# Strided attention on one Trainium2 core: longer read runs in the DMAs that load Q and store the output

## The chip, the cores and the metric

The kernel runs on one core of one Trainium2 chip. The metric is the device time of one execution in microseconds (us), as the median of several executions. The kernel before took 130.86 us (median of 3 runs, 130.84 to 131.28).

## The reference, cut to what matters

Every query attends to the 16 keys at positions 0, 64, 128, ... of its head. Q, K, V and the result are float32 of shape (8, 12, 1024, 64), so Q and the result are 25.17 MB each. Of K and V only one row in 64 is read.

```python
attend_positions = np.arange(0, seq, stride)          # stride = 64: 16 positions
k = K[:, :, attend_positions, :];  v = V[:, :, attend_positions, :]
scores = np.einsum('bhqd,bhkd->bhqk', q, k) / np.sqrt(dim)
weights = softmax(scores)                             # over the 16 keys
result[:, :, i, :] = np.einsum('bhqk,bhkd->bhqd', weights, v)
```

## The kernel before

The 96 heads are worked in 24 groups of four. A group's Q is 1 MiB: each of the 128 SBUF partitions gets 32 rows of 64 floats, 8 KiB in one piece. There are 11 buffers for Q and 9 for results. All 11 first loads are issued before any computing; from then on the program issues a store and a load in turn.

```python
QBUFS = 11
OBUFS = 9
# ... pools, constants, K and V: cut ...

def load(g):                       # 128 runs of 8 KiB, HBM and SBUF alike
    qn[g] = qn_pool.tile([P, 32 * D], FP32, name="qn", tag="qn")
    nc.sync.dma_start(qn[g], _ap_with(Q, [[32 * D, P], [1, 32 * D]], g * HG * SD))

for g in range(QBUFS):
    load(g)
# ... transposes (PE, evicted by ACT), scores (PE, exp by ACT), sums, outputs (PE, scaled by DVE): cut ...

def store(g):                      # 256 runs of 4 KiB, SBUF and HBM alike
    nc.sync.dma_start(
        _ap_with(out, [[16 * D, P], [2 * SD, 2], [1, 16 * D]], g * HG * SD),
        out_sb[g].rearrange("p b i x -> p b (i x)"),
    )

for g in range(NG):
    # ... sums(g), outputs(g, 0..3), scores(g + 1), transposes(g + 2): cut ...
    store(g)
    if g + QBUFS < NG:
        load(g + QBUFS)
```

A *run* here is one contiguous piece that one side of a DMA reads or writes. For a load the read side is HBM (the chip's main memory) and the write side is SBUF (the core's own memory, in 128 partitions); for a store it is the other way round. A *packet* is one record of the profiler for one piece of a DMA on one of the core's 16 DMA engines. PE, ACT and DVE are the engines that compute (matmul, activation, vector).

The softmax here doesn't subtract the row's maximum and nothing guards it: scores larger than these inputs give would overflow.

## Time and profile before

| what | before | where it is read |
|---|---|---|
| time, median | 130.86 us | timed runs |
| DMA data queue, share of 16 engines' span | 97.6% | part 3 of the page |
| ACT, DVE, PE busy | 67%, 65%, 55% | part 1 of the page |
| last byte moved | 127.8 us | DMA packet records |
| last DVE instruction ends | 114 us | timeline |

Lines of the page of the kernel before: the span; the busy share of the DMA engines in 40 slices, in tenths, and the GB/s of each slice; the packets by size; the data queue; the chain of waits by engine; two groups of instructions (busy us, mean ns); and the two kinds of DMA with the time from issue to landing.

```profile
span 129.1 us, 2215 instructions
...
DMA  2999999999999999999999999999999999999980
GB/s 64 273 426 416 419 431 419 421 411 421 415 423 433 405 428 426 414 425 420 419 428 420 416 435 419 419 431 415 420 434 404 420 417 417 419 420 421 420 360 34
DMA packets 13098, 51.26 MB, mean 397 GB/s; under 512 B 3872, under 2 KB 3872, under 8 KB 10016
...
q1 hardware_dynamic: 13088, 51.12, 97.6%
...
ACT 61%; PE 11%; DVE 5%; DMA 3%; issue 3%; POOL 3%; ACTq 1%; DVEq 0%; POOLq 0%
...
L223 DVE TENSOR_TENSOR out_sb<-o_ps,rec 128x512 f32<-128x512 f32 x96 | 63.2, 689 | 15.2 <-PE o_ps L218 12.8
L178 ACT COPY qt<-qt_ps 128x1024 bf16<-128x1024 bf16 x48 | 46.2, 1015 | 5.2 <-PE qt_ps L173 4.7
...
qn<-in_Q_dram SPq DMA_DIRECT2D x24, 1024.0 KB, 19.5
out_dram<-out_sb SPq DMA_DIRECT2D x24, 1024.0 KB, 19.2
```

The DMA row stands at 9 from slice 2 almost to the end: nothing else is full for so long. The chain of waits names ACT for 61%, but ACT and DVE are finished by 114 us while stores, issued 19 us ahead of their landing, are still draining.

Busy time by stage in the kernel before. Each line is one stretch: its limits and length, then busy us and instructions of each engine, granted TensorE clock, DMA share and GB/s.

```profile
core 0: us, PE busy (x) PEld busy (x) DVE busy (x) ACT busy (x) POOL busy (x), PEclk, DMA share, GB/s
12.00:24.00 12.00, 7.74 (x66) 5.50 (x65) 8.43 (x16) 6.63 (x8) 0.00 (x0) 0.88 1.02 424
60.00:95.00 35.00, 23.42 (x317) 17.48 (x315) 26.87 (x45) 30.19 (x37) 0.00 (x0) 1.00 1.02 423
112.00:122.00 10.00, 0.90 (x4) 0.22 (x2) 2.06 (x4) 0.00 (x0) 0.00 (x0) 0.50 1.02 420
```

The three stretches are the loads-only stage, the mixed stage and the stores-only stage. The DMA share is 1.02 in each. It can exceed 1 because the records of neighbouring packets overlap by about 4 ns: a 4 KiB packet's record lasts 159 ns, and the next packet of its engine starts after 155 ns (median).

These GB/s count a packet whole in the stretch in which it starts. That is coarse for long packets, so all rates from here on are worked out from the packet records of the data queue (q1), with each packet's bytes spread evenly over its recorded time. For the kernel before they are 421.8, 421.5 and 420.5 GB/s in these stretches. There was no idle engine to fill: from 12 to 122 us the records never show fewer than 16 packets under way. In that time a gain could come only from the pace, which was 155 ns from start to start for 4 KiB, and for 8 KiB 309 ns in the loads-only and 306 ns in the mixed stage (medians). How high the rate could go was not shown.

### The profile page before, as it was taken

To read this page: it belongs to the slowest core of one execution; us is meant where nothing else is said; L and a number is where in the kernel's file an instruction comes from. 1 tells how busy PE (TensorE), PEld (TensorE's weight loads), DVE (VectorE), ACT (ScalarE), POOL (GpSimd) and SP (SyncE) were. 2 spreads that over 40 slices of the span, in tenths; PEclk is the share of its full clock that TensorE was granted. 3 is DMA by queue.
4 is the path that set the end of the run, shared out by engine and by line. 5 is a ranking of instruction groups with operands and counts; after the bars stand their busy time and mean duration, and the time that the engine had idled before them with its cause. 6 is when DMAs were issued, how large, how long until landed. Compare 5 with 4: busy or idle time off the path is not lost.

```text
span 129.1 us, 2215 instructions
## 1 busy us (share of the span) xinstructions
PE 70.4 (55%) x880; PEld 51.8 (40%) x880; DVE 83.7 (65%) x144; ACT 86.2 (67%) x103; POOL 5.1 (4%) x23
## 2 busy tenths in 40 slices
PE   0071665986666776666866667856668765600000
PEld 0040542765444554445655445544456543300000
DVE  6229964787778777778777787777787777830000
ACT  2173294988889888889888899888898888200000
POOL 4460000000000000000000000000000000000000
PEclk9999997799999999999999999999999999555555
DMA  2999999999999999999999999999999999999980
GB/s 64 273 426 416 419 431 419 421 411 421 415 423 433 405 428 426 414 425 420 419 428 420 416 435 419 419 431 415 420 434 404 420 417 417 419 420 421 420 360 34
DMA packets 13098, 51.26 MB, mean 397 GB/s; under 512 B 3872, under 2 KB 3872, under 8 KB 10016
## 3 DMA queue, kind: packets, MB, share of 16 engines
q1 hardware_dynamic: 13088, 51.12, 97.6%
q8 instruction: 7, 0.11, 0.3%
q14 instruction: 3, 0.02, 0.0%
HBM read 25.95 MB, written 25.17 MB: 396 GB/s over the span
## 4 chain that ended last, share of the span: by engine, by line
ACT 61%; PE 11%; DVE 5%; DMA 3%; issue 3%; POOL 3%; ACTq 1%; DVEq 0%; POOLq 0%
ACT qt L178 34%; ACT w L198 27%; PE sc L186 8%; DVE v_bd L160 3%; DMA k_raw<-in_K_dram 3%; PE qt_ps L173 1%; DVE out_sb L223 1%; POOL k_dup L96 1%; PE o_ps L218 1%; POOL perm_v L100 1%; POOL v_bf L104 1%; ACTq L285 1%; PE sm L207 1%; DVEq L285 0%; PE vp L155 0%
## 5 line engine op out<-in xcount | busy, mean ns | idle before, releaser
L223 DVE TENSOR_TENSOR out_sb<-o_ps,rec 128x512 f32<-128x512 f32 x96 | 63.2, 689 | 15.2 <-PE o_ps L218 12.8
L178 ACT COPY qt<-qt_ps 128x1024 bf16<-128x1024 bf16 x48 | 46.2, 1015 | 5.2 <-PE qt_ps L173 4.7
L198 ACT ACTIVATE w<-sc 64x512 bf16<-64x512 f32 x48 | 35.3, 736 | 13.1 <-PE sc L186 12.8
L218 PE MATMUL o_ps<-v_bd,w 128*128 128x256 bf16 x192 | 34.2, 284 | 0.0
L173 PE MATMUL qt_ps<-identity,qn 128*128 128x128 bf16 x384 | 31.1, 228 | 0.2 <-ACT qt L178 0.2
L173 PEld LDWEIGHTS <-qn 128*128 128x128 bf16 x384 | 27.3, 103 | 3.9 <-issue 2.6
L186 PE MATMUL sc<-qt,k_t 128*32 128x512 bf16 x96 | 9.8, 396 | 24.3 <-ACT qt L178 24.3
L218 PEld LDWEIGHTS <-w 128*128 128x128 bf16 x192 | 14.6, 100 | 6.6 <-issue 5.6
L186 PEld LDWEIGHTS <-k_t 128*32 128x32 bf16 x96 | 4.4, 93 | 29.1 <-issue 29.0
L211 DVE RECIPROCAL rec<-sm 128x32 f32<-128x32 f32 x24 | 8.6, 358 | 9.0 <-PE sm L207 8.9
L207 PE MATMUL sm<-s_sel,w 128*128 128x4 bf16 x192 | 8.5, 166 | 6.7 <-ACT w L198 5.6
L207 PEld LDWEIGHTS <-w 128*128 128x128 bf16 x192 | 6.4, 96 | 10.8 <-ACT w L198 10.8
L160 DVE TENSOR_SCALAR v_bd<-vp,mask 128x384 bf16<-128x384 f32 x16 | 8.5, 608 | 0.1
L146 ACT CAST k_t<-kp 64x512 bf16<-64x512 f32 x6 | 3.5, 579 | 3.5 <-PE kp L140 3.4
L140 PE MATMUL kp<-perm_k,k_dup 128*128 128x128 bf16 x12 | 1.5, 312 | 6.6 <-POOL k_dup L96 6.6
L155 PE MATMUL vp<-v_bf,perm_v 128*128 128x384 bf16 x4 | 1.8, 491 | 4.6 <-DVE v_bd L160 4.1
L140 PEld LDWEIGHTS <-k_dup 128*128 128x128 bf16 x12 | 1.2, 145 | 6.6 <-POOL k_dup L96 6.6
L118 DVE TENSOR_SCALAR slot_i<-iota_p 128x1 int16<-128x1 int16 x1 | 0.2, 156 | 4.6 <-POOL iota_p L116 4.6
L146 ACT ACT_TABLE_LOAD x1 | 1.3, 1283 | 2.5 <-DVE k_t L107 2.5
L107 DVE MEMSET k_t<- 128x1536 uint32 x1 | 1.3, 1338 | 1.1 <-PEq L271 1.1
L155 PEld LDWEIGHTS <-perm_v 128*128 128x128 bf16 x4 | 0.5, 128 | 3.7 <-issue 3.7
L96 POOL CAST k_dup<-k_raw 128x768 bf16<-128x768 f32 x2 | 1.6, 827 | 3.0 <-DMA k_raw<-in_K_dram 3.0
(15 smaller groups left out, 6.0 us busy)
## 6 DMA issues: line engine op xcount, KB each, us to landing
qn<-in_Q_dram SPq DMA_DIRECT2D x24, 1024.0 KB, 19.5
out_dram<-out_sb SPq DMA_DIRECT2D x24, 1024.0 KB, 19.2
k_raw<-in_K_dram SPq DMA_DIRECT2D x1, 384.0 KB, 4.2
v_raw<-in_V_dram SPq DMA_DIRECT2D x1, 384.0 KB, 5.4
```

Source lines behind the costliest of these rows:

```text
L96: nc.gpsimd.tensor_copy(out=k_dup[:, :, e], in_=k_raw)
L140: nc.tensor.matmul(kp[:, i], lhsT=k_dup[:, 4 * n + i].rearrange("p e d -> p (e d)"), rhs=pk, start=True, stop=True,)
L146: nc.scalar.copy(k_t[h, 4 * n : 4 * n + 4, :, :, e].rearrange("p n c s k -> p (n c s) k"), kp[h].rearrange("p n c s k -> p (n c s) k"),)
L160: nc.vector.tensor_scalar(out=v_bd[:, 6 * n : 6 * n + 6, c, s], in0=vp, scalar1=mask[:, s : s + 1], scalar2=None, op0=ALU.mult,)
L173: nc.tensor.transpose(ps[:, i], _ap_with(qb, [qb.ap[0], [2, P]], extra_offset=(8 * x + i) * 2 * P + 1), identity,)
L178: nc.scalar.copy(qt[g][:, x], ps)
L186: nc.tensor.matmul(sc[32 * j : 32 * j + 32], lhsT=kt[:, 32 * j : 32 * j + 32], rhs=_ap_with(q, [q.ap[0], [P, 8], [8 * P, 2], [1, 32]], ext ...
L198: nc.scalar.activation(out=_ap_with(wa, [wa.ap[0], [P, 8], [1, 2], [2, 32]], extra_offset=64 * a), in_=sc[64 * a : 64 * a + 64].rearrange( ...
L207: nc.tensor.matmul(sm[:, :, i], lhsT=wt[g][:, i], rhs=s_sel, start=True, stop=True)
L211: nc.vector.reciprocal(rec[g], sm.rearrange("p b i e -> p b (i e)"))
L218: nc.tensor.matmul(ps[:, :, i], lhsT=wt[g][:, 2 * c + i], rhs=v_bd[:, g // 2, g % 2].rearrange("p s d -> p (s d)"), start=True, stop=True,)
L223: nc.vector.tensor_tensor(out=out_sb[g][:, :, 4 * c : 4 * c + 4], in0=ps.rearrange("p b i (e d) -> p b (i e) d", e=2), in1=rec[g][:, :, 4 ...
```

## The change

The intent is to spend fewer read runs on the same bytes. Loads read 32 KiB runs: four partitions' rows are contiguous in HBM, so one read feeds four writes of 8 KiB. Stores read the whole 8 KiB of a partition, and it is written as two runs of 4 KiB. Bytes, write runs, order, buffers and every computing instruction stay. The instruction is built by hand because the ordinary call did not keep the long read: in the kernel before, a store's 8 KiB lie in one piece in each partition, and yet the stores are recorded as 6,144 packets of 4 KiB.

```diff
--- before.py
+++ after.py
@@ -19,6 +19,24 @@
 def _ap_with(ap: bass.AP, new_ap, extra_offset: int = 0) -> bass.AP:
     return dataclasses.replace(
         ap, ap=[list(p) for p in new_ap], offset=ap.offset + extra_offset
+    )
+
+
+def _copy(nc, out: bass.AP, in_: bass.AP):
+
+    sides = [
+        mybir.BassSymbolicTensorAccessPattern(
+            ap=side.ap, dtype=side.dtype, bass_ap=side,
+            is_dma=True, for_custom_bir_dma=True,
+        )
+        for side in (in_, out)
+    ]
+    return nc.sync.add_instruction(
+        mybir.InstDMACopy(
+            name=nc.get_next_instruction_name(), engine=mybir.EngineType.SP,
+            ins=sides[:1], outs=sides[1:], queue="qSPDynamicHW",
+            mode="Copy",
+        )
     )
 
 
@@ -75,7 +93,9 @@
 
     def load(g):
         qn[g] = qn_pool.tile([P, 32 * D], FP32, name="qn", tag="qn")
-        nc.sync.dma_start(qn[g], _ap_with(Q, [[32 * D, P], [1, 32 * D]], g * HG * SD))
+        _copy(
+            nc, qn[g], _ap_with(Q, [[HG * SD // 32, 32], [1, HG * SD // 32]], g * HG * SD)
+        )
 
     for g in range(QBUFS):
         load(g)
@@ -228,9 +248,11 @@
         )
 
     def store(g):
-        nc.sync.dma_start(
+        o = out_sb[g]
+        _copy(
+            nc,
             _ap_with(out, [[16 * D, P], [2 * SD, 2], [1, 16 * D]], g * HG * SD),
-            out_sb[g].rearrange("p b i x -> p b (i x)"),
+            _ap_with(o, [o.ap[0], [1, 1], [1, 32 * D]]),
         )
 
     for g in range(2):
```

## The prediction

> **What bounds the kernel now.** DMA. The slice row shows the 16 DMA engines at 9 tenths or more from about 6 us to 124 us, and the stage table gives a DMA share of 1.01 to 1.02 in all four stages I cut: 421 GB/s at 10–25 us (loads only), 418 at 25–40, 422 at 40–95 (loads and stores mixed), 419 at 98–124 (stores only). The queue table gives the one data queue 51.12 MB and 97.6% of 16 engines' span. ACT (67%), DVE (65%) and PE (55%) finish early: the last DVE instruction ends near 114 us, while DMA moves until 127.8 us. The printed chain of waits runs through ACT for 61% of the span, but it ends in DMA work still queued; ACT's 3.94 us per group times 24 is 94.5 us, less than the streaming time. Start-up (about 6 us, K and V in 256 B runs) and the end are fixed.
>
> **What the change does.** Bytes, write runs, order, buffers and every compute instruction stay. Read runs go from 3072 of 8 KiB to 768 of 32 KiB for loads, and from 6144 of 4 KiB to 3072 of 8 KiB for stores.
>
> **Cost of a run.** In the DMA packet records a 4096 B packet lasts 159 ns and an 8192 B packet 309 ns: 150 ns per 4 KiB plus about 9 ns. Records overlap, so I take start-to-next-start on one engine: 155 ns and 306 to 307 ns. That is 151.5 ns per 4 KiB and about 4 ns per packet (256 B packets come every 14 ns, also 4 to 5 ns over their bytes). [...]
>
> If this cost belongs to the read run, it is saved 2304 + 3072 = 5376 times: 5376 × 4.5 ns / 16 = 1.5 us, all of it on the critical path because DMA is the bound. If it belongs to the write run, nothing is saved. The upper bound is every loss: 50.3 MB at 151 ns per 4 KiB on 16 engines is 116 us, against 120.8 us now; at most 4 to 5 us, and semaphore writes, instruction fetches (16 KiB, 0.9 to 1.1 us each) and uneven engines at the end (the last packets of the engines spread over about 3 us) keep part of that. Compute, 94.5 us from about 18 us, stays hidden.
>
> **Predicted time: 129.5 us** (−1%), range 127.6 to 131.4. Chances: faster by over 2% 0.16, within 2% 0.74, slower by over 2% 0.10.
>
> **What would show it right.** Compute groups unchanged in count and mean. GB/s in the mixed and store stages up by 1 to 1.5%, to about 426. If packets are recorded by read run, the data queue falls from 13,088 to about 7,700 packets, with 32 KiB at about 1.21 us and 8 KiB stores at about 306 ns. The last landing comes about 1.5 us earlier. If packets stay 4 and 8 KiB with the same periods, the cost sits on the write side and the time stays at 130.9.
>
> **What would make it wrong.** Slower: 32 long reads may be dealt to the engines otherwise than 128 rows, [...] or a read feeding four writes may stall between them; DMA would then stay "busy" at lower GB/s. Faster: if the loads-only excess (311 to 312 ns per packet in places, against 306) or the uneven finish also comes from short reads, 3 us could go. The trace can't separate read cost from write cost, since their runs pair one to one today.

The forecast's 4.5 ns were read from packet records of the kernel before.

## The result, and the profile after

The change took 130.32 us (median of 4 runs, 130.26 to 130.36), the kernel before 130.87 us in the same rounds (4 runs). The ratio is 0.995 with a 95% interval of 0.993 to 0.9971: a gain of half a per cent that is clear of noise. A ratio is the mean time of one kernel's fast runs over that of the other's of the same rounds, so not quite the ratio of the medians quoted.

The same lines of the page of the changed kernel:

```profile
span 128.5 us, 2215 instructions
...
DMA  2999989999899899999999999999998999999980
GB/s 57 351 398 418 449 367 490 388 423 439 339 421 487 357 441 439 413 434 449 383 467 426 393 459 428 393 469 421 405 469 357 416 434 416 421 428 421 434 337 23
DMA packets 7722, 51.26 MB, mean 399 GB/s; under 512 B 3872, under 2 KB 3872, under 8 KB 3872
...
q1 hardware_dynamic: 7712, 51.12, 96.3%
...
ACT 60%; PE 13%; DVE 5%; DMA 3%; POOL 3%; issue 2%; ACTq 1%; DVEq 0%; POOLq 0%
...
L243 DVE TENSOR_TENSOR out_sb<-o_ps,rec 128x512 f32<-128x512 f32 x96 | 63.3, 688 | 15.3 <-PE o_ps L238 12.9
L198 ACT COPY qt<-qt_ps 128x1024 bf16<-128x1024 bf16 x48 | 46.2, 1015 | 5.2 <-PE qt_ps L193 4.7
...
qn<-in_Q_dram SPq DMA_DIRECT2D x24, 1024.0 KB, 19.0
out_dram<-out_sb SPq DMA_DIRECT2D x24, 1024.0 KB, 19.5
```

The packets fell from 13,088 to 7,712 on the data queue. A packet is therefore recorded by read run. The DVE and ACT groups are what they were (688 against 689 ns, 1015 ns in both). The GB/s row is jagged now only because 32 KiB packets are counted where they start.

The same stretches of the changed kernel, with the same columns:

```profile
core 0: us, PE busy (x) PEld busy (x) DVE busy (x) ACT busy (x) POOL busy (x), PEclk, DMA share, GB/s
12.00:24.00 12.00, 7.59 (x65) 5.31 (x65) 8.51 (x16) 6.48 (x8) 0.00 (x0) 0.87 1.02 429
60.00:95.00 35.00, 23.54 (x320) 17.59 (x316) 26.72 (x45) 30.22 (x36) 0.00 (x0) 1.00 1.02 430
112.00:122.00 10.00, 0.38 (x2) 0.10 (x1) 2.23 (x4) 0.00 (x0) 0.00 (x0) 0.55 1.01 425
```

DMA is as full as before. With the bytes spread, the rates are:

| stage | before | after | change |
|---|---|---|---|
| loads only, 12 to 24 us | 421.8 GB/s | 422.8 | +0.2% |
| mixed, 60 to 95 us | 421.5 | 425.2 | +0.9% |
| stores only, 112 to 122 us | 420.5 | 425.2 | +1.1% |

The mixed and stores-only stages gained 0.9 and 1.1%, where 1 to 1.5% was expected, and the loads-only stage hardly anything. Between 12 and 122 us the packet records of both kernels never show fewer than 16 packets under way, so no idle engine shows in that time: the gain is in the pace of the engines and not in fewer gaps. From the moment when 13 MB had been moved to that of 50 MB the kernel before took 88.16 us and the changed one 87.32 us: 0.84 us saved. By the mean landing of the last store over the 16 engines 0.74 us is left (126.12 to 125.38 us), and by its last engine 0.63 us (128.13 to 127.50 us).

### The profile page after: what moved, and what is told of

Same layout as the page of the kernel before. It is cut to its first block, busy times and chain, and to the rows that moved or that the text cites. A ratio compares the mean times of both kernels' runs of the same rounds, so it can differ in the third digit from the quotient of the medians.

```text
span 128.5 us, 2215 instructions
## 1 busy us (share of the span) xinstructions
PE 69.4 (54%) x880; PEld 51.1 (40%) x880; DVE 83.7 (65%) x144; ACT 86.3 (67%) x103; POOL 5.1 (4%) x23
## 3 DMA queue, kind: packets, MB, share of 16 engines
q1 hardware_dynamic: 7712, 51.12, 96.3%
## 4 chain that ended last, share of the span: by engine, by line
ACT 60%; PE 13%; DVE 5%; DMA 3%; POOL 3%; issue 2%; ACTq 1%; DVEq 0%; POOLq 0%
ACT qt L198 34%; ACT w L218 26%; PE sc L206 8%; DVE v_bd L180 3%; DMA k_raw<-in_K_dram 3%; PE qt_ps L193 2%; PE o_ps L238 2%; DVE out_sb L243 1%; POOL k_dup L116 1%; POOL perm_v L120 1%; PE sm L227 1%; POOL v_bf L124 1%; ACTq L307 1%; DVEq L307 0%; PE vp L175 0%
## 5 line engine op out<-in xcount | busy, mean ns | idle before, releaser
L198 ACT COPY qt<-qt_ps 128x1024 bf16<-128x1024 bf16 x48 | 46.2, 1015 | 5.2 <-PE qt_ps L193 4.7
L238 PE MATMUL o_ps<-v_bd,w 128*128 128x256 bf16 x192 | 33.4, 278 | 0.6 <-DVE out_sb L243 0.6
```

The costliest lines, as they stand in the source:

```text
L198: nc.scalar.copy(qt[g][:, x], ps)
L238: nc.tensor.matmul(ps[:, :, i], lhsT=wt[g][:, 2 * c + i], rhs=v_bd[:, g // 2, g % 2].rearrange("p s d -> p (s d)"), start=True, stop=True,)
```

## The experiments

Theory P is the prediction's: a read run costs about 4.5 ns wherever it is, and write runs are free. Its rivals changed as results came in: the cost is on the write runs (S, then W), the time is given back at the end by an engine that lags (E, U), and the cost lies on the SBUF side of a DMA (B). Each kernel was profiled once, so a figure from packet records is one profile's. The diffs are cut short: loads_wide, stores_wide, loads16k_stores_wide and the pairs are shown against the change, loads_write1k against the kernel before, and the others against the experiment that stands before them (loads_write4k against loads_write1k, stores_write1k against stores_wide). Medians of the kernel before were 130.90, 130.83 and 130.87 us.

### loads_wide: the loads' half of the change

```diff
 def store(g):
-    o = out_sb[g];  _copy(nc, ..., _ap_with(o, [o.ap[0], [1, 1], [1, 32 * D]]))
+    nc.sync.dma_start(..., out_sb[g].rearrange("p b i x -> p b (i x)"))   # as before
```

> Only the loads read 32 KiB runs; stores are those of before. Theory P (the prediction's: every read run costs about 4.5 ns, write runs are free): 2304 fewer read packets x 4.5 / 16 = 0.65 us saved, 130.2 us. Theory S (the 4.5 ns of a run pair is split, about 2.5 ns read side and 2 ns write side, and the loads-only stage is held near 422 GB/s by something else): 0.15 to 0.25 us saved, 130.65 us, loads-only stage (10 to 24 us) still at 422 GB/s. Theory E (the long packets give time back through uneven engines at the end): 0 or a loss, 130.9 us, with the spread of the 16 engines at a landing wider than before's 1.7 us in the mixed stage.

It took 130.86 us; the ratio is 0.9995 (0.9976 to 1.0013). The loads-only stage ran at 422.0 GB/s. From 13 to 50 MB it took 87.84 us, 0.32 us less than before. The last engine landed 2.43 us after the mean of the 16, against 2.01 us in the kernel before, so the last landing did not come earlier at all. Theory P's 0.65 us is not there. Theory E looked right in this one profile; it is tested again below. Its other sign, a wider spread of the 16 engines at the landings of the mixed stage (60 to 95 us), was hardly there: 1.85 us in the median, against 1.71 in the kernel before.

### stores_wide: the stores' half of the change

```diff
 def load(g):
-    _copy(nc, qn[g], _ap_with(Q, [[HG * SD // 32, 32], [1, HG * SD // 32]], g * HG * SD))
+    nc.sync.dma_start(qn[g], _ap_with(Q, [[32 * D, P], [1, 32 * D]], g * HG * SD))   # as before
```

> Only the stores read 8 KiB runs; loads are those of before. Theory P: 3072 x 4.5 / 16 = 0.86 us saved, 130.0 us. Theory S: 3072 x 2.5 to 3 / 16 = 0.5 to 0.6 us saved, 130.3 us. Theory E: as fast as the whole change or faster than it (130.1 to 130.3 us), because the uneven finish that the 32 KiB loads bring is absent (spread at landings stays 1.7 us).

It took 130.51 us; the ratio is 0.9972 (0.996 to 0.9984). From 13 to 50 MB it took 87.48 us, 0.68 us less. 23.4 MB of stores lie in that stretch, or 2,850 removed read runs: 0.68 us x 16 / 2,850 = 3.8 ns each. Its loads-only stage ran at 422.1 GB/s. So most of the change's gain is the stores'. The lag of its last engine was 2.17 us, so theory E's sharp form (as fast as the whole change) did not come true.

### loads_write1k: short write runs, reads as before

```diff
 def load(g):
-    nc.sync.dma_start(qn[g], _ap_with(Q, [[32 * D, P], [1, 32 * D]], g * HG * SD))
+    q = qn[g]
+    _copy(nc, _ap_with(q, [q.ap[0], [256, 8], [1, 256]]),
+          _ap_with(Q, [[32 * D, P], [1, 1], [1, 32 * D]], g * HG * SD))
```

> Loads read 8 KiB runs as before but write 1 KiB runs: 21504 more write runs in all, no more read runs. Theory P: no change, 130.9 us, packets of 309 ns. Theory S: 21504 x 2 / 16 = 2.7 us more, 133.5 us, load packets longer by about 7 x 2 = 14 ns (309 to about 323).

It took 141.39 us; the ratio is 1.0799. The loads-only stretch:

```profile
core 0: us, PE busy (x) PEld busy (x) DVE busy (x) ACT busy (x) POOL busy (x), PEclk, DMA share, GB/s
12.00:24.00 12.00, 8.20 (x66) 5.63 (x65) 8.41 (x16) 6.58 (x8) 0.00 (x0) 1.00 1.02 349
```

348.2 GB/s with the bytes spread. Both theories were far off: the write run is not free and does not cost 2 ns. At 348.2 GB/s an engine needs 16 x 8192 / 348.2 = 376.4 ns for 8 KiB with eight write runs; the kernel before needs 16 x 8192 / 421.8 = 310.7 ns with one. By an estimate from these two runs an added write run costs, while only loads run, (376.4 - 310.7) / 7 = 9.4 ns.

### loads_both1k: short write runs and short reads

```diff
-          _ap_with(Q, [[32 * D, P], [1, 1], [1, 32 * D]], g * HG * SD))
+          _ap_with(Q, [[32 * D, P], [256, 8], [1, 256]], g * HG * SD))
```

> Loads read and write 1 KiB runs: 21504 more pairs. Both theories: 21504 x 4.5 / 16 = 6 us more, 136.9 us, 24576 packets of 1 KiB. The difference to loads_write1k is the read run's own cost: theory P 6 us (4.5 ns), theory S about 3.3 us (2.5 ns).

It took 141.54 us; the ratio is 1.0813. Its loads-only stretch, and the packet line of its page:

```profile
core 0: us, PE busy (x) PEld busy (x) DVE busy (x) ACT busy (x) POOL busy (x), PEclk, DMA share, GB/s
12.00:24.00 12.00, 7.89 (x67) 5.74 (x67) 8.46 (x16) 6.79 (x9) 0.00 (x0) 0.90 1.10 348
```

```profile
DMA packets 34602, 51.26 MB, mean 367 GB/s; under 512 B 3872, under 2 KB 28448, under 8 KB 34592
```

The packets rose to 34,602, so the reads really were short, and the rate is 348.2 GB/s as in loads_write1k; in the mixed stage it is 392.0 against 392.1. With write runs of 1 KiB, eight times as many read runs on the HBM side cost nothing measurable. (The opposite mixture, short reads into long writes, could not be built. The compiler refused three forms for loads and one for stores. So it stays untested.)

### loads_write4k: the new rule at another size

```diff
-    _copy(nc, _ap_with(q, [q.ap[0], [256, 8], [1, 256]]),
+    _copy(nc, _ap_with(q, [q.ap[0], [1024, 2], [1, 1024]]),
```

> Loads read 8 KiB runs as before, write 4 KiB runs. Theory W (new, from the 1 KiB runs: while only loads run, [...] 9.4 ns for each write run, and read runs are hidden behind that): [...] 409.6 GB/s at 12 to 20 us, against 421.9 of before; mixed stage about 7 ns per added run; in all 3072 x 7 to 9 / 16 = 1.3 to 1.7 us more, 132.4 us. Theory S (2 ns per write run): 0.4 us more, 131.3 us, 419 GB/s.

Two terms of theory W are cut here, a rate for the bytes and the sum made with it. The sum came to 320 ns for 8 KiB, and so to 409.6 GB/s. The two runs above give nearly the same: 310.7 + 9.4 = 320.1 ns with two write runs, or 409.5 GB/s.

It took 132.12 us; the ratio is 1.0096 (1.008 to 1.0112). Its loads-only stretch:

```profile
core 0: us, PE busy (x) PEld busy (x) DVE busy (x) ACT busy (x) POOL busy (x), PEclk, DMA share, GB/s
12.00:24.00 12.00, 8.19 (x65) 5.62 (x65) 8.58 (x16) 6.40 (x8) 0.00 (x0) 1.00 1.01 410
```

409.7 GB/s with the bytes spread, where theory W said 409.6. In the mixed stage the two runs cost less: 419.0 GB/s against 421.5, which is 3.7 ns per added write run in place of the 7 expected. So the 9.4 ns, taken from the rates at 8 and 1 KiB, hold in the loads-only stage at 4 KiB too, and there theory W explains why longer reads brought next to nothing (422.8 GB/s against 421.8): the write runs, which the change leaves alone, set the pace.

### loads16k_stores_wide: half as long read runs in the loads

```diff
-    _copy(nc, qn[g], _ap_with(Q, [[HG * SD // 32, 32], [1, HG * SD // 32]], g * HG * SD))
+    _copy(nc, qn[g], _ap_with(Q, [[HG * SD // 64, 64], [1, HG * SD // 64]], g * HG * SD))
```

> The change, but loads read 16 KiB runs instead of 32 KiB. Theory U (the time that the loads' long runs save on average is given back because the last engine lags more behind the others with longer packets): 130.1 to 130.3 us, mean landing of the last store over the 16 engines 125.4 us, last engine less than 2.1 us behind that. Without U: 130.35 to 130.45 us, between stores_wide alone and the change, since only two thirds of the read runs are saved that the change saves.

It took 130.33 us; the ratio is 0.9962 (0.9949 to 0.9975). The mean landing was 125.43 us and the last engine 1.97 us behind. This cannot be told from the change, nor the two hypotheses from each other: inconclusive.

### stores_write1k: short write runs in the stores

```diff
 def store(g):
-    ... _ap_with(out, [[16 * D, P], [2 * SD, 2], [1, 16 * D]], g * HG * SD),
+    ... _ap_with(out, [[32 * D, P], [256, 8], [1, 256]], g * HG * SD),      # rows in wrong places
```

> Wrong output on purpose (a group's 1 MiB lands contiguously, so the rows are in the wrong places): stores read 8 KiB runs and write 1 KiB runs, 18432 more write runs than stores_wide. If write runs of a store cost 2 ns: +2.3 us on stores_wide, 132.8 us. If they cost 9.4 ns as in the loads: +10.8 us, 141.3 us. If they are free (prediction's theory P): 130.5 us.

It took 131.68 us with the wrong output; the ratio is 1.0065. The stores-only stage (112 to 122 us) ran at 404.7 GB/s against 425.9 in stores_wide: 323.9 against 307.8 ns for 8 KiB, or 2.7 ns for each of six added write runs. From 13 to 50 MB it took 2.33 us more than stores_wide, as expected at 2 ns per run (2.2 ns each in that stretch), but by the ratios to the kernel before the time rose by only about 1.2 us (0.93% of 130.85): its last engine landed 0.92 us after the mean, in stores_wide 2.17 us. So a write run of a store costs 2 to 3 ns, much less than the 9.4 ns of a write run in the loads-only stage. The output's placement differs from stores_wide too, and what that does by itself was not measured.

### stores_both1k: short reads in the stores as well

```diff
-    _ap_with(o, [o.ap[0], [1, 1], [1, 32 * D]]),
+    _ap_with(o, [o.ap[0], [256, 8], [1, 256]]),
```

> Wrong output on purpose, as stores_write1k: stores read and write 1 KiB runs. If read runs of a store cost 3 to 4 ns beside the write runs: 21504 x 3.5 / 16 = 4.7 us more than stores_write1k. If the slower side alone sets the pace, as in the loads: same as stores_write1k.

It took 136.84 us (wrong output); the ratio is 1.0459. That is 5.16 us more than stores_write1k, over 21,504 more read runs: 5.16 x 16 / 21,504 = 3.8 ns per read run, the same as the 3.8 ns found from 4 to 8 KiB. In a store the read runs cost, and they add to the write runs; in a load with short writes they do not. The stores-only stage of the two, stores_write1k first:

```profile
112.00:122.00 10.00, 0.93 (x5) 0.20 (x2) 2.48 (x4) 0.00 (x0) 0.00 (x0) 0.50 1.01 406
112.00:122.00 10.00, 0.38 (x2) 0.10 (x1) 2.13 (x4) 0.00 (x0) 0.00 (x0) 0.55 1.06 367
```

With the bytes spread these are 404.7 and 366.6 GB/s, or 323.9 and 357.5 ns for 8 KiB: 4.8 ns for each of seven added read runs. So 3.8 ns is an average over stages and not a constant.

### change_again and loads_wide_again: was the lagging engine chance?

Both kernels are unaltered copies, run beside each other on another chip, so there is no diff to show.

> The change itself, unaltered, beside the others of this call: 130.3 us; mean landing of the last store over the 16 engines 125.4 us (0.7 us before that of the kernel before), the last engine 2.0 to 2.2 us behind that mean.

Four runs took 130.19 to 130.34 us; the ratio of these to before is 0.9957 (0.9944 to 0.9971). The fifth, which was the profiled one, took 325.96 us. In it the TensorE transposes took 714 ns each in place of 227 and PE was busy for 95% of the span; DMA was not the bound: ACT's copies of the transposes waited 134.4 us for PE, and DVE's scaling 157.8 us. It shares nothing with the question here, and it is left out of every comparison. The landings that were expected could not be read from it, so that half of the expectation stays unanswered.

> Only the loads wide, a second profile and five more rounds. If long load packets make the last engine lag more (theory U): 130.85 us again, last engine again 2.3 us or more behind the mean landing, against 2.0 in before. If the lag of the first profile was chance: 130.5 to 130.6 us, lag near 2.0 us.

It took 130.65 us, between the two forecasts; the ratio is 0.9988 (0.9975 to 1.0002), and the last engine landed 1.90 us after the mean. Theory U's lag at the end did not come again: the 2.43 us of the first profile was no property of long packets. In the mixed stage the engines did land further apart this time, 2.56 us in the median; the change has 2.33, and stores_wide, without long loads, 1.81. Whether long load packets spread the engines there is open, for the two profiles of this one kernel differ by 0.7 us. From 13 to 50 MB it took 87.87 us, 0.29 us less than before (0.32 the first time), and the loads-only stage again showed no gain. So the loads' half is worth about 0.3 us of streaming, and by the two ratios 0.07 and 0.16 us of time, neither clear of noise.

### pairs_read16k and pairs_read8k: still longer reads in the stores

The store takes two groups at once, so that 16 KiB per partition are contiguous in SBUF; the control has the same stores with two reads of 8 KiB.

```diff
-    OBUFS = 9
+    OBUFS = 4                                    # buffers of two groups
-            out_sb[g] = out_pool.tile([P, 2, 16, D], FP32, ...)          # every group
+            out_sb[g // 2] = out_pool.tile([P, 2, 2, 16, D], FP32, ...)  # every second group
-    _ap_with(out, [[16 * D, P], [2 * SD, 2], [1, 16 * D]], g * HG * SD),
-    _ap_with(o, [o.ap[0], [1, 1], [1, 32 * D]]),
+    _ap_with(out, [[16 * D, P], [2 * SD, 4], [1, 16 * D]], g * 2 * HG * SD),
+    _ap_with(o, [o.ap[0], [1, 1], [1, 64 * D]]),          # pairs_read16k
+    _ap_with(o, [o.ap[0], [32 * D, 2], [1, 32 * D]]),     # pairs_read8k
     # ... index of out_sb in the scaling, and store(g // 2) after every second group: cut ...
```

> The change, with two groups per store (2 MiB): reads of 16 KiB runs from SBUF, writes of 4 KiB as ever; 4 output buffers of two groups in place of 9 of one. Theory B (a DMA pays for the runs on its SBUF side: write runs of a load, read runs of a store; the HBM side is nearly free): 1536 fewer read runs than the change, x 3.9 / 16 = 0.37 us less than pairs_read8k, stores-only rate 425 to 426 GB/s against 423. Rival (the gain of the wide stores was in the number of packets that start a 4 KiB write each, and ends once the read is longer than one write): no difference to pairs_read8k.

> Control of pairs_read16k: the same two-group stores, read as two 8 KiB runs per partition. Stores-only rate as the change's, 423 GB/s; time that of the change plus or minus what two-group stores cost in buffers and at the end (estimate: 0 to 0.5 us more).

pairs_read16k took 130.09 us, ratio 0.9941 (0.9928 to 0.9953); pairs_read8k 130.28 us, ratio 0.9956 (0.9943 to 0.9968). Between 108 and 122 us they stored at 424.5 and 423.4 GB/s. The difference has the sign that theory B expected and about half its size (0.19 us in place of 0.37; 0.18 us from 13 to 50 MB, or 2.0 ns per removed read run), and the intervals overlap: it is not settled whether a read run costs as much when it already spans two writes. pairs_read16k has the lowest median, but it is not clear of the change, whose interval overlaps its own.

## Why the prediction was right or wrong

**Right: the bound.** DMA set the time before and after (its data queue took 97.6 and 96.3% of 16 engines' span), and computing stayed hidden with groups of unchanged duration (DVE 689 and 688 ns, ACT 1015 ns in both). The packet count and the 32 KiB packets (1.219 us in the median of the mixed stage, 1.21 predicted) came as foretold. The time, 130.32 us, lies in the range of 127.6 to 131.4 us and in the class "within 2%", but both also held no change at all (130.87 us), so that says little for the mechanism.

**Wrong: the saving.** The failed step is the prediction's "If this cost belongs to the read run, it is saved 2304 + 3072 = 5376 times: 5376 × 4.5 ns / 16 = 1.5 us, all of it on the critical path". Measured were 0.55 us. It failed in three terms:

1. *Not every removed read run was being paid for.* In the loads-only stage, where 11 of the 24 loads stream, the write runs of 8 KiB set the pace: 9.4 ns per added write run, estimated from the rates at 8 and 1 KiB, foretold the rate at 4 KiB (409.5 GB/s against 409.7), while with write runs of 1 KiB, reads of 1 KiB in place of 8 changed nothing (348.2 GB/s in both). Those loads hold 11 x 96 = 1,056 of the removed runs, 0.30 us of the sum. The time from 2 to 10.5 MB shows what came of it: 20.22 to 20.25 us in four profiles with 8 KiB reads, 20.14 to 20.21 in five with 32 KiB.
2. *The price was set too high.* The prediction read "about 4 ns" from its own trace and then multiplied by 4.5. stores_wide and stores_both1k give 3.8 ns per read run of a store on average; for the loads in the mixed stage, 13 x 96 = 1,248 removed runs between 13 and 50 MB, loads_wide and its repeat give 0.32 and 0.29 us, which is 4.1 and 3.8 ns. For the other 4,320 runs, at 3.8 ns, that is about 0.19 us less, which leaves about 1.0 us.
3. *The two halves did not add up fully, and the ends kept some.* From 13 to 50 MB, most of what follows the loads-only stage, the stores' half saved 0.68 us, the loads' half 0.32 and 0.29 us, and both together 0.84 us. The two profiles of loads_wide differ by 0.03 us, less than the 0.14 us that is missing here, but the others are single profiles. In the mixed stage a 32 KiB load packet took 1,219 ns in the change and 1,213 ns in loads_wide; why is open. Of the 0.84 us the mean landing kept 0.74 and the last engine 0.63.

The prediction offered a choice, read run or write run, and gave both sides one price. The runs show neither: in a store the read run costs about 3.8 ns and the write run 2 to 3 ns on top; while only loads run the write run costs 9.4 ns and the read run hides behind it; in the mixed stage a load's read run costs about as much as a store's.

**Wrong: two side remarks.** It was thought that the loads-only excess (311 to 312 ns per packet) might come from short reads; it does not. It was also said that an 8 KiB store packet would be recorded at about 306 ns; its start-to-start time was 307 ns but its record 311 ns. The record of a packet and the pace of an engine are different things.

**Shown, and only argued.** That write runs pace the loads-only stage and that store reads cost about 3.8 ns on average is shown by the runs. That the reason is the SBUF side in both cases (SBUF is written in a load and read in a store) fits all of this, but no run reversed it: a store with short SBUF reads into long HBM writes could not be built, and the paired stores gave no clear answer. It is also open why write runs cost less in the mixed stage (3.7 ns per added run at 4 KiB, and 6.8 ns at 1 KiB, from 4.94 us over the 11,648 added runs between 13 and 50 MB of loads_write1k).

The end needs a caution. In every profile of a fast run the last engine lands its share of the last store 0.9 to 2.4 us after the mean of the 16, and that engine sets the time. This lag moved by about half a microsecond between two profiles of the same kernel (2.43 and 1.90 us in the loads-only half), as much as the whole gain looked for.

## What to carry to other kernels

Ask of a DMA-bound stage which side's runs set its pace before lengthening the other's: vary each side alone, because a trace in which reads and writes pair one to one cannot tell them apart. Lengthening SBUF reads of stores paid here (0.68 us from 13 to 50 MB), lengthening HBM reads of loads hardly did (0.32 and 0.29 us). When the gain is near half a per cent, compare the time between two byte counts in the middle of the stream as well as the end, for one late engine can hide it (here it landed 0.9 to 2.4 us after the mean).
